# Attention scores: the low parts of the keys on both halves of the partitions, so that both score products read 128 rows

## The chip, the cores and the metric

One core of a Trainium2 chip runs the kernel. The metric is the device time of one execution in microseconds (us). Engines are named as in the profile: PE (TensorE; PEld are its weight loads), DVE (VectorE), ACT (ScalarE), POOL (GpSimd) and SP (SyncE, which issues most transfers).

## What is computed

Two layers of a mixer (convolution and a recurrent scan) with a feed-forward part come first; then a block of attention and a block of 32 experts, of which each token takes four. All data is float32. The change lies in the attention of the second block, over 512 queries and 768 keys (512 tokens and 256 of context). Cut to what matters:

```
scale = d ** -0.5                                    # d = 64
def block(qi):                                       # 8 heads, 2 key heads
    s = jnp.einsum('bhgqd,bkhd->bhgqk', qi, k, preferred_element_type=jnp.float32) * scale
    p = jax.nn.softmax(s, axis=-1)
    return jnp.einsum('bhgqk,bkhd->bqhgd', p.astype(v.dtype), v)
```

There are two kinds of attention: a grouped-query one as above, and a differential one (4 heads), in which two softmaxes of 64 channels each are subtracted, the second times a factor lambda, before the product with the values.

## The kernel before

Queries and keys lie with the channel on the partition: a tile of 128 partitions holds two heads (or the two parts of a differential head) of 64 channels. `s` (or `z`) says which half of the partitions.

PE multiplies in float32r, which keeps fewer bits than float32. So each operand is split into a high part (rounded to float32r) and a low part (what is left). `split_q` makes the tile QS, [128, 2, 512]: for each half `s` the high parts on the half's own 64 partitions and the low parts on the other 64. `split_k` makes KS, [128, 2, 768]: for each half the keys' high parts on both halves of the partitions (two copies, by POOL or, for the first head, by ACT, lines 1475 and 1476), and KL, [128, 768]: the low parts, each half on its own partitions (DVE, line 1477). Both tiles have two buffers.

`softmax` makes the scores of 128 queries against 768 keys, in three pieces of 256 keys, each as two products that add up. The first (line 1488) contracts over 128 rows: high and low queries against high keys. The second (line 1489) contracts over 64 rows: high queries against low keys, `T.matmul(sc[:, N], q[R, s, Q], kl[R, N], ...)`, where R are the half's own partitions. The scores lie in the PSUM tile `sc`, which has two buffers. DVE then takes the least of each row (line 1491; the queries carry -1/8), ACT the exponential with its row sum (line 1494), DVE the reciprocal.

What follows a score step: DVE scales the probabilities P (line 1528, or 1557 and 1558 for a differential head, where two steps are merged), PE transposes them (line 1503, `tp`), ACT copies the transposes into PT (line 1504), and PE multiplies PT with the values into `av` (line 1535 for the grouped-query steps, with 64 columns of weights, line 1565 for the differential heads).

`attention` lists 64 score steps: four differential heads of 8 steps, then four grouped-query steps `j` of 8 steps. What follows a step is emitted three steps later; the scheduler of the framework then orders each engine's instructions. Attention is thus 64 x 6 = 384 score products. A key tile is split five times in all: once for each differential head and once for all grouped-query steps.

Ahead of attention are the products for queries, keys and values; behind it the output projection, the routing, and the experts, whose weights stream from DRAM for the rest of the time.

Of the kernel before, what the change touches and what calls it, by code (L numbers as in the profile page):

```python
# [8 lines left out]
F32 = mybir.dt.float32  # L9
F32R = mybir.dt.float32r  # L10
# [11 lines left out]
DEC = 0.606531  # L22


# ---------------------------------------------------------------- host layout
class Vecs:
    """Per-channel vectors side by side, channel on the partition."""
# [19 lines left out]
def pack_m(w):  # L47
    """[K, M] -> [M/128, 128, K/128 * 128]: the k-tiles of one column block side by side."""
    k, m = w.shape
    return np.ascontiguousarray(  # L50
        w.reshape(k // 128, 128, m // 128, 128).transpose(2, 1, 0, 3).reshape(m // 128, 128, -1))


def host(I):
# [26 lines left out]
    for l in range(2):  # L81
# [8 lines left out]
        up = np.stack([I["decay_up"][l], I["iclr_up"][l]], 0)               # [2, dir, 64, 512]  # L90
# [6 lines left out]
    qa = w[:, :512].reshape(1024, 2, 4, 64).transpose(0, 2, 1, 3).reshape(1024, 512)   # heads (j, 4 + j) side by side  # L97
# [63 lines left out]
def consts():  # L161
    """Depend on shapes alone."""
# [20 lines left out]
# ---------------------------------------------------------------- the kernel  # L183
# [4 lines left out]
class Stat:  # L188
    """sums of squares over the channels, a column per 128 tokens, from tiles as they come"""
# [24 lines left out]
class Kern:  # L214
    def __init__(self, tc, A, pvat, out, dbg=None):
        self.tw, self.narrow = NT, False
        self.tc, self.nc, self.A, self.at, self.out = tc, tc.nc, A, pvat, out
        self.dbg_out = dbg or {}
        self.V, self.S, self.G, self.T = tc.nc.vector, tc.nc.scalar, tc.nc.gpsimd, tc.nc.tensor
        self.moe_ps, self.queue, self.spare, self.wpre = False, None, [], []  # L220
        self.ada_w = 1024
        self.th = ""               # the strand of work that emits: buffers are handed out in order within each
        self.phm, self.ppm, self.psh = {}, {}, {}     # pools of a strand of its own

    # -- small helpers
# [39 lines left out]
    def rsqrt(self, t, n, name):  # L265
        """t[128, n] > 0 -> 1/sqrt(t), by bits and three Newton steps."""
# [15 lines left out]
    def pin(self, ins):  # L282
        """behind what its engine was given before"""
        return self.tc.keep_in_program_order(ins)
# [11 lines left out]
    # -- weights  # L296
# [18 lines left out]
    def dense(self, src, act, segs, done, kts=8, m=128):  # L315
        """out[m, tok] = w^T act in three passes of float32r; done(i, seg, psum)."""
# [14 lines left out]
    def flush(self, g, mid=None):  # L331
        """the products put off: the first g side by side, a term of each in turn; mid: emitted after their weights;
        what it returns: a step of it per term, done before the last"""
# [20 lines left out]
    # -- adaLN: columns of silu(c) @ w + b, both streams  # L354
# [10 lines left out]
    def ada(self, w, cs, bname, mod, groups, pth=None):  # L365
        """mod[128, 48, 2] += for the groups of 2048 columns."""
        for g in groups:
# [15 lines left out]
            # column q*128 + 32 j + s of tp: block 4 j + q of the group, stream s  # L383
# [8 lines left out]
    # -- rms norm and modulation, channel-major  # L392
    def modcols(self, mod, gname, sh, sc, name):
        """a = g (1 + sc), b = sh for both streams: [128, 8, 2]."""
# [5 lines left out]
    def normstat(self, tiles, segs, name):  # L400
        """1 / rms, on all partitions"""
# [18 lines left out]
    def spread(self, r, segs, name):  # L420
        """a column per 128 tokens as rows on all partitions"""
# [10 lines left out]
    def normmod(self, tiles, segs, a, b, name, streams=None, full=False, dst=None, bcs=None, ahead=False):  # L432
        """hi/lo of rms(x) a + b (full: itself, in dst where given)."""
# [43 lines left out]
    def normmod2(self, tiles, ms, g, a, b):  # L477
        """hi/lo of rms(xb) a + b with xb = rms(x) g, over the latents; then xb in x's place.
        rms(xb)'s mean square is that of x g over the mean square of x; ms: both."""
# [35 lines left out]
    # -- group norm over the 64-channel groups of a tile, tokens at the offsets of segs  # L515
    def gn_center(self, t, segs, name, pin=False):
        """t -= group mean (in place)."""
# [7 lines left out]
    def grp_rstd(self, sq, segs, scale, eps, name, floor=None, rb=None):  # L525
        """psum per seg: rsqrt(sum over the tile's two 64-channel groups * scale + eps)."""
# [23 lines left out]
    # -- token shift of width 3  # L550
# [13 lines left out]
    def wi_tile(self, l, mt, segs, name, out=None):  # L564
        """one column block of the RWKV part of u, shifted. mt counts blocks of 128 after the conv part.
        Where the product is put off, what shifts it."""
# [20 lines left out]
    # -- the scan of one head pair, both directions. Per chunk of 64 tokens:  # L587
    #    A, B (alpha with beta, kappa), D, E (rho with beta, kappa), X = (1 + A)^-1,
    #    U = -X (alpha S + B V), y = rho S + D U + E V, S' = f (S + beta U + kappa V);
    #    with W = X alpha and U0 = -X B V that is S' = M S + c, y = R S + y0 where  # L590
    #    M = f (1 - beta W), c = f (beta U0 + kappa V), R = rho - D W, y0 = D U0 + E V
    def units(self, d, q):
        """first chunk of the direction's batch q"""
# [6 lines left out]
    def scan_in(self, l, hp, kvs, kt=None, rt=None, kk=None):  # L600
# [9 lines left out]
        off = (self.ph if hp % 2 else ph).tile([128, 24, 32], F32, name="off", bufs=1)      # rows 0-31, 64-95: the block beside the diagonal  # L610
# [21 lines left out]
        for d in range(2):  # L632
# [15 lines left out]
            V.tensor_scalar(thw, thw, -0.5 * DEC, -0.5 * DEC, op0=ALU.mult, op1=ALU.add)   # log decay  # L648
# [28 lines left out]
            # kappa = Eb k (1 + (a - 1) ka), beta = Eb kk a, a = (1 + tha) / 2  # L677
# [11 lines left out]
            # A, for the reverse direction with alpha's token on the partition; its diagonal 32 x 32 blocks go to  # L689
            # lane 8 b + 4 s + i of quadrant (direction, half)  # L690
# [19 lines left out]
    def scan_inv(self, inv=None):  # L710
# [3 lines left out]
        # inverses of the 32 x 32 blocks, one block to a partition  # L714
# [19 lines left out]
    def scan_x(self, off, G1, G2):  # L734
        V, S, G, T = self.V, self.S, self.G, self.T
        # X transposed: diagonal blocks, and -(T2 A21 T1)^T (forward), -(T1 A12 T2)^T (reverse)
# [34 lines left out]
    def scan_pre(self, l, hp, H):  # L771
        """per chunk M and R (over alpha and rho), c and y0"""
# [8 lines left out]
        def early(q, d):  # L781
# [9 lines left out]
            # the two heads on two halves of the rows, side by side  # L791
# [16 lines left out]
            # f beta and f kappa with the token on the partition  # L808
# [10 lines left out]
            # f on the diagonal in alpha's place  # L819
# [69 lines left out]
    def scan_run(self, l, hp, H):  # L889
        """the recurrence over chunks, both directions in step"""  # L890
# [4 lines left out]
        for q in range(3):  # L895
            full = l == 0 or q > 0
            ub = [self.units(d, q) for d in range(2)]
            # the half of the batch with the smaller chunk numbers first
# [30 lines left out]
    def scan_out(self, l, hp, y, kvs, segs, out=None):  # L929
        """group norm, bonus and gate, in place; the last pair's into out"""  # L930
# [31 lines left out]
    def token_terms(self, l, hp, kt, vt, rt, kvs, segs):  # L962
        """normed removal key, bonus of the current token and gate, to DRAM"""
# [4 lines left out]
        # v with the token on the partition  # L968
# [38 lines left out]
    def conv_z(self, l, ci, segs):  # L1007
        """value * sigmoid(gate) (twice), zero-padded: x at 15, ctx at 557."""
# [26 lines left out]
    def conv_taps(self, l, ci, z, segs, pool):  # L1035
        """the depthwise convolution"""
# [20 lines left out]
    def conv_norm(self, l, ci, tiles, segs, mixd):  # L1057
        """twice the silu of the group norm"""
# [21 lines left out]
    def project(self, l, kvs, mixd, zd, lw):  # L1080
        """w_in and the token shift"""
# [9 lines left out]
        # high and low parts over each other: [hi; lo] of w, [lo; hi] of a  # L1091
# [41 lines left out]
    def conv_diag(self, l, ci, zd, segs, steps):  # L1133
        """the depthwise convolution as products with diagonals, in steps"""
# [76 lines left out]
    def mixer_out(self, l, kvs, mixd, mod, spill):  # L1211
        """x + gt1 (mix @ w_out)"""
# [53 lines left out]
    def ffn(self, l, xt, r2, a2, b2, mod):  # L1266
        """x + gt2 (swiglu), in place; the hidden columns in three parts."""
# [56 lines left out]
    # ------------------------------------------------------------ second block  # L1324
# [4 lines left out]
    def rope(self, t, out, name):  # L1329
        """t [128, 512] of the latents -> out"""  # L1330
# [8 lines left out]
    def head_norm(self, t, segs, g):  # L1339
        """rms over the 64 channels of each head, in place."""  # L1340
# [7 lines left out]
    def ctx_ahead(self, mod):  # L1348
        """the second block's normed context"""
# [8 lines left out]
    def qkv(self, xt, ms, mod):  # L1358
        """x (after the first block's norm), queries, keys and token-major values."""
# [25 lines left out]
        def piped(jobs):  # L1385
            """two products ahead of what follows one"""
# [21 lines left out]
        def lat(i):  # L1408
            def first():
# [4 lines left out]
                self.dense(self.A["wqkv"][i], hx, xs, done)    # 0-3 qa, 4 ka, 5-8 qb, 9-12 kb  # L1414
# [22 lines left out]
    def lambda_col(self):  # L1437
        """[128, 1]: minus lambda"""
# [17 lines left out]
    def split_q(self, q, first=False):  # L1456
        """times -1/8, per head, high parts on its own partitions and low parts on the others"""
# [10 lines left out]
    def split_k(self, k, first=False):  # L1468
        """per head, high parts on both halves of the partitions; low parts"""
        t = self.pqs.tile([128, 2, NT], F32R, name="KS", bufs=2)  # L1470
        lo = self.pqs.tile([128, NT], F32R, name="KL", bufs=2)
        for s in range(2):
# [4 lines left out]
            self.V.tensor_tensor(lo[R], k[R], t[R, s].bitcast(F32), ALU.subtract)  # L1477
        return t, lo

    def softmax(self, q, k, s, qt):  # L1480
        """unnormalised exp of the scores of 128 queries and 1 / row sum; the queries carry -1/8, so that the
        scores' maximum is the least here"""
        V, S, T = self.V, self.S, self.T
        kh, kl = k
        Q, R = slice(qt * 128, (qt + 1) * 128), slice(64 * s, 64 * s + 64)
        sc = self.psc.tile([128, NT], F32, name="sc")       # starts on a bank or in its middle
        for N in (slice(0, 256), slice(256, 512), slice(512, 768)):
            T.matmul(sc[:, N], q[:, s, Q], kh[:, s, N], start=True, stop=False)  # L1488
            T.matmul(sc[:, N], q[R, s, Q], kl[R, N], start=False, stop=True)  # L1489
# [17 lines left out]
    def attention(self, mod):  # L1507
# [3 lines left out]
        steps = []           # (scores and exp, what follows) in order  # L1511
# [108 lines left out]
    def rows_ahead(self, mod):  # L1620
        """scale, shift and gate of the experts' norm as rows in DRAM; the router's part that all tokens share"""
        V, S, G, T, nc, A = self.V, self.S, self.G, self.T, self.nc, self.A
        # the sum of what the experts make of a token, zero at first
# [30 lines left out]
    def out_proj(self, mix, mod):  # L1654
        """Output projection and residual, token-major in Y; what the routing needs of it, as the tiles come:
        the mean squares, and the products with the router's weights before the norm's scale of a token."""
# [793 lines left out]
```

## Time and profile before

| | us |
|---|---|
| three runs | 4617.17, 4621.3, 4623.69 |
| median | 4621.3 |
| profiled execution, first to last instruction | 4622.1 |
| of it PE busy (share) | 4289.2 (93%) |
| DVE busy | 2919.9 (63%) |
| ACT busy | 2070.3 (45%) |
| POOL busy | 963.8 (21%) |

The span of the profiled execution is the one time that is known of it; it lies among the three runs. Busy shares over the whole span mix stages with different limits, so they are read by stage. Attention takes about 287 us of the span.

### The profile page before, as it was taken

What the parts mean: (1) busy time and instruction counts of PE and PEld (TensorE: products, weight loads), DVE (VectorE), ACT (ScalarE), POOL (GpSimd) and SP (SyncE); (2) the same over time, 40 slices, a digit from 0 to 9 for tenths busy, and PEclk for the clock granted to TensorE, in tenths of its full rate; (3) what the DMA queues carried; (4) which work ended last, traced back from release to release, by engine and by line L of the source; (5) the groups of instructions that cost most, each with busy time, mean ns of one, the idle gap of its engine ahead of it and who ended that gap; (6) DMA issues with size and microseconds to landing.
All of it is one profiled execution on the core that took longest, in us unless ns stands there. A gap on an engine that the chain in (4) does not pass through costs nothing.

```text
span 4622.1 us, 68704 instructions
## 1 busy us (share of the span) xinstructions
PE 4289.2 (93%) x26930; PEld 3276.4 (71%) x26930; DVE 2919.9 (63%) x4417; ACT 2070.3 (45%) x3140; POOL 963.8 (21%) x796
## 2 busy tenths in 40 slices
PE   7888999999999888899899999998899999999997
PEld 5664565888888664455788886666777777777775
DVE  6884675433333884755444355645888888888887
ACT  4554332231212553432323242343566666766665
POOL 1552121000000441111000032102323223323222
PEclk9888999999999998889999998798999999999998
DMA  4224323311112224322332241003799989999896
GB/s 157 69 90 128 103 88 107 106 60 64 64 61 80 69 86 134 92 88 84 116 105 92 87 146 41 3 1 126 239 306 305 309 300 303 306 309 304 306 303 244
DMA packets 249438, 691.04 MB, mean 150 GB/s; under 512 B 52055, under 2 KB 60912, under 8 KB 249106
## 3 DMA queue, kind: packets, MB, share of 16 engines
q1 hardware_dynamic: 224354, 636.25, 40.9%
q0 software_dynamic: 7808, 20.74, 1.9%
q10 hardware_dynamic: 16944, 29.58, 1.9%
q8 instruction: 214, 3.51, 0.3%
q14 instruction: 118, 0.97, 0.1%
HBM read 643.12 MB, written 51.45 MB: 150 GB/s over the span
## 4 chain that ended last, share of the span: by engine, by line
PE 42%; DMA 6%; DVE 3%; issue 1%; ACT 1%; POOL 0%; SPq 0%; DVEq 0%; POOLq 0%; ACTq 0%
DMA yd<-ye,ixs 5%; PE dps L326 4%; PE dps L328 4%; PE dps L327 4%; PE acc L1930 4%; PE acc L1931 4%; PE acc L1929 4%; PE acc L1953 3%; PE acc L1954 3%; PE acc L1952 3%; PE tok L1872 2%; PE sc L1489 2%; PE sc L1488 1%; PE av L1535 1%; PE tp L1503 1%; DVE elo L1911 1%
## 5 line engine op out<-in xcount | busy, mean ns | idle before, releaser
L1909 ACT CAST ehi<-eraw 128x1024 fp32r<-128x1024 f32 x768 | 803.1, 1051 | 381.4 <-PE acc L1931 229.3
L1911 DVE TENSOR_TENSOR elo<-eraw,ehi 128x1024 fp32r<-128x1024 f32 x640 | 865.3, 1390 | 97.7 <-ACT ehi L1909 95.5
L309 ACT CAST whi<-wraw 128x1024 fp32r<-128x1024 f32 (+1 forms) x234 | 239.5, 1028 | 768.1 <-PE dps L327 416.0
L1911 POOL TENSOR_TENSOR elo<-eraw,ehi 128x1024 fp32r<-128x1024 f32 x128 | 331.3, 2588 | 847.8 <-ACT ehi L1909 771.8
L310 DVE TENSOR_TENSOR wlo<-wraw,whi 128x1024 fp32r<-128x1024 f32 (+1 forms) x234 | 292.2, 1251 | 225.6 <-ACT whi L309 222.3
L1930 PE MATMUL acc<-elo,ex 128*128 128x512 f32 x1024 | 416.0, 406 | 14.4 <-DVE elo L1911 13.2
L1929 PE MATMUL acc<-ehi,ex 128*128 128x512 f32 x1024 | 408.7, 399 | 0.3 <-ACT ex L1875 0.3
L1931 PE MATMUL acc<-ehi,ex 128*128 128x512 f32 x1024 | 408.0, 398 | 0.0
L327 PE MATMUL dps<-h2l,whi 128*128 128x512 f32 x992 | 351.2, 354 | 0.0
L326 PE MATMUL dps<-h2h,whi 128*128 128x512 f32 x992 | 351.1, 354 | 0.0
L328 PE MATMUL dps<-h2h,wlo 128*128 128x512 f32 x992 | 350.3, 353 | 0.0
L1930 PEld LDWEIGHTS acc<-elo,ex 128*128 128x128 f32 x1024 | 194.7, 190 | 65.4 <-DVE elo L1911 20.6
L376 PE MATMUL adaps<-wraw,cs 128*32 128x512 f32 x576 | 234.6, 630 | 2.8 <-DMA wraw<-in_ada_dram 1.8
L1929 PEld LDWEIGHTS acc<-ehi,ex 128*128 128x128 f32 x1024 | 194.7, 190 | 47.3 <-issue 0.7
L328 PE MATMUL dps<-hh,wlo 128*128 128x512 f32 (+3 forms) x568 | 209.5, 370 | 17.6 <-DVE wlo L310 17.6
L1931 PEld LDWEIGHTS acc<-ehi,ex 128*128 128x128 f32 x1024 | 194.6, 190 | 39.3
L326 PE MATMUL dps<-hh,whi 128*128 128x512 f32 (+3 forms) x568 | 210.4, 370 | 5.5 <-ACT whi L309 4.9
L1953 PE MATMUL acc<-elo,eah 128*128 128x512 f32 x512 | 206.9, 404 | 1.7 <-DVE elo L1911 1.7
L326 PEld LDWEIGHTS dps<-h2h,whi 128*128 128x128 f32 x992 | 188.0, 190 | 26.4
L327 PE MATMUL dps<-hl,whi 128*128 128x512 f32 (+3 forms) x568 | 206.8, 364 | 0.0
L1952 PE MATMUL acc<-ehi,eah 128*128 128x512 f32 x512 | 203.5, 397 | 3.3 <-DVE ye L1972 3.3
L328 PEld LDWEIGHTS dps<-h2h,wlo 128*128 128x128 f32 x992 | 187.8, 189 | 26.1
(605 smaller groups left out, 9508.8 us busy)
## 6 DMA issues: line engine op xcount, KB each, us to landing
eraw<-in_ewi_dram SPq DMA_DIRECT2D x503, 512.0 KB, 6.0
eraw<-in_ewo_dram SPq DMA_DIRECT2D x256, 512.0 KB, 5.2
wraw<-in_ada_dram SPq DMA_DIRECT2D x256, 256.0 KB, 2.9
wraw<-in_wi_dram SPq DMA_DIRECT2D x44, 512.0 KB, 3.8
wraw<-in_wg_dram SPq DMA_DIRECT2D x44, 512.0 KB, 3.7
wraw<-in_wu_dram SPq DMA_DIRECT2D x44, 512.0 KB, 3.7
wraw<-in_wd_dram SPq DMA_DIRECT2D x32, 512.0 KB, 3.7
wraw<-in_wqkv_dram SPq DMA_DIRECT2D x28, 512.0 KB, 3.7
```

The source lines that it names most:

```text
L309: self.S.copy(hi, raw)
L310: i = self.V.tensor_tensor(lo, raw, hi.bitcast(F32), ALU.subtract)
L326: self.T.matmul(ps, w0, h[:, o:o + n], start=k == 0, stop=False)
L327: self.T.matmul(ps, w0, l[:, o:o + n], start=False, stop=False)
L328: self.T.matmul(ps, w1, h[:, o:o + n], start=False, stop=k == kts - 1)
L1909: self.S.copy(hi, raw)
L1911: (self.G if self.wn % 6 == 0 else self.V).tensor_tensor(lo, raw, hi.bitcast(F32), ALU.subtract)
L1929: T.matmul(acc[:, N], xh[:, K], wh[:, W], start=False, stop=False)
L1930: T.matmul(acc[:, N], xh[:, K], wl[:, W], start=False, stop=False)
L1931: T.matmul(acc[:, N], xl[:, K], wh[:, W], start=False, stop=k == 7)
L1952: T.matmul(acc[:, N], ah[:, K], wh[:, N], start=k == 0, stop=False)
L1953: T.matmul(acc[:, N], ah[:, K], wl[:, N], start=False, stop=False)
```

## The change

DVE now writes the low parts of the keys on both halves of the partitions: KL becomes [128, 2, 768], and in place of one subtraction of 64 partitions per half there are two with the same inputs, one for each place. The second score product reads all 128 rows of QS and KL, so that it also adds low queries against low keys. The rest of the difference drops comments and moves line numbers: from line 1478 on, a line of the changed kernel is one higher than in the kernel before (the products at lines 1488 and 1489 stand at 1489 and 1490, the subtraction at 1478).

```
     def split_k(self, k, first=False):
         t = self.pqs.tile([128, 2, NT], F32R, name="KS", bufs=2)
-        lo = self.pqs.tile([128, NT], F32R, name="KL", bufs=2)
+        lo = self.pqs.tile([128, 2, NT], F32R, name="KL", bufs=2)
         for s in range(2):
             R, N = slice(64 * s, 64 * s + 64), slice(64 - 64 * s, 128 - 64 * s)
             C = lambda e: self.S.copy if e else self.G.tensor_copy
             C(first)(t[R, s], k[R])
             C(False)(t[N, s], k[R])
-            self.V.tensor_tensor(lo[R], k[R], t[R, s].bitcast(F32), ALU.subtract)
+            for P in (R, N):
+                self.V.tensor_tensor(lo[P, s], k[R], t[R, s].bitcast(F32), ALU.subtract)
         return t, lo
...
         kh, kl = k
-        Q, R = slice(qt * 128, (qt + 1) * 128), slice(64 * s, 64 * s + 64)
+        Q = slice(qt * 128, (qt + 1) * 128)
...
             T.matmul(sc[:, N], q[:, s, Q], kh[:, s, N], start=True, stop=False)
-            T.matmul(sc[:, N], q[R, s, Q], kl[R, N], start=False, stop=True)
+            T.matmul(sc[:, N], q[:, s, Q], kl[:, s, N], start=False, stop=True)
```

How the instructions stand now, in two places. DVE at the start of attention, before the change (QS and KL are the split queries and keys, `nb` the row minimum, `wlo` a weight of the output projection that is prepared early):

```order
L1465 SCALAR_TENSOR_TENSOR QS<-q_22701,QS 64x512 x2
L1477 TENSOR_TENSOR KL<-k_22706,KS 64x768 x2
L310 TENSOR_TENSOR wlo<-wraw,whi 128x1024
L1491 TENSOR_REDUCE nb<-sc 128x1
L310 TENSOR_TENSOR wlo<-wraw,whi 128x1024
L1491 TENSOR_REDUCE nb<-sc 128x1
L1465 SCALAR_TENSOR_TENSOR QS<-q_22702,QS 64x512
```

The same place in the changed kernel:

```order
L1465 SCALAR_TENSOR_TENSOR QS<-q_22701,QS 64x512 x2
L1478 TENSOR_TENSOR KL<-k_22706,KS 64x768 x4
L310 TENSOR_TENSOR wlo<-wraw,whi 128x1024 x2
L1492 TENSOR_REDUCE nb<-sc 128x1
L1465 SCALAR_TENSOR_TENSOR QS<-q_22702,QS 64x512
L1492 TENSOR_REDUCE nb<-sc 128x1
L1465 SCALAR_TENSOR_TENSOR QS<-q_22702,QS 64x512
```

The first key tile's four subtractions stand ahead of the first reduction, where there were two, and the second weight has moved ahead of the first reduction.

PE near the end of the second differential head, before (`sc` the scores, `tp` the transposes, `av` the product with the values):

```order
L1488 MATMUL sc<-KS,QS 128x256
L1489 MATMUL sc<-KL,QS 128x256
L1503 MATMUL tp<-ct,P 128x128 x3
L1565 MATMUL av<-PT,vtok 128x256 x3
L1503 MATMUL tp<-ct,P 128x128 x3
L1565 MATMUL av<-PT,vtok 128x256 x3
L1488 MATMUL sc<-KS,QS 128x256
L1489 MATMUL sc<-KL,QS 128x256
```

The same place in the changed kernel:

```order
L1489 MATMUL sc<-KS,QS 128x256
L1490 MATMUL sc<-KL,QS 128x256
L1566 MATMUL av<-PT,vtok 128x256 x6
L1504 MATMUL tp<-ct,P 128x128 x6
L1489 MATMUL sc<-KS,QS 128x256
L1490 MATMUL sc<-KL,QS 128x256
```

The same products stand there, but those with the values come as one group ahead of the transposes rather than in two groups between them; the score products keep their pairs.

## Rows read from the trace of the kernel before

**Rows 1.** The page's first line: the whole span.

```profile
span 4622.1 us, 68704 instructions
```

**Rows 2.** Busy time by stage: length, each engine, granted clock, DMA share, GB/s.

```profile
2846.00:3018.00 172.00, 155.81 (x493) 106.64 (x491) 103.60 (x195) 64.13 (x130) 28.75 (x25) 0.68 0.04 11
3018.00:3133.00 115.00, 115.00 (x518) 70.53 (x518) 54.12 (x105) 52.20 (x115) 12.46 (x16) 0.97 0.04 12
...
3205.00:3330.00 125.00, 99.30 (x468) 81.07 (x468) 99.51 (x112) 65.40 (x87) 53.19 (x24) 0.86 0.53 174
3330.00:4590.00 1260.00, 1214.53 (x5690) 976.81 (x5690) 1045.45 (x949) 861.27 (x978) 377.30 (x151) 0.99 0.90 307
```

**Rows 3.** The chain of waits, 2840 to 3135 us, shares by line.

```profile
by line: PE sc L1489 23.7%; PE sc L1488 20.5%; PE av L1535 15.4%; PE tp L1503 15.4%; PE av L1565 12.4%; PE tp L1589 2.0%; ACT P L1494 2.0%; DVE nb L1491 1.3%; PE tp L1580 1.2%; DVE QS L1465 0.9%; PE dps L328 0.6%; ACT PT L1504 0.6%; PE dps 
```

**Rows 4.** DVE's groups, 2846 to 3018 us: busy, mean ns, idle before, releaser.

```profile
L1491 DVE TENSOR_REDUCE nb<-sc 128x1 f32<-128x768 f32 x38 | 36.4, 958 | 61.3 <-PE sc L1489 61.2
...
L1477 DVE TENSOR_TENSOR KL<-k,KS 64x768 fp32r<-64x768 f32 x10 | 10.9, 1086 | 0.2
```

**Rows 5.** PE in order of time, second half: start us, length us, instruction.

```profile
3047.89 0.38 PE L1489 MATMUL sc<-KL,QS 64*128 64x256 f32 x1
3048.20 0.39 PE L1488 MATMUL sc<-KS,QS 128*128 128x256 f32 x1
3048.52 0.38 PE L1489 MATMUL sc<-KL,QS 64*128 64x256 f32 x1
```

**Rows 6.** PE in order of time, dense products ahead of attention, full clock.

```profile
2721.03 0.28 PE L328 MATMUL dps<-hch,wlo 128*128 128x256 f32 x1
2721.15 0.28 PE L326 MATMUL dps<-hch,whi 128*128 128x256 f32 x1
2721.27 0.28 PE L327 MATMUL dps<-hcl,whi 128*128 128x256 f32 x1
```

**Rows 7.** PE in order of time, first half, half clock.

```profile
2910.75 0.58 PE L1489 MATMUL sc<-KL,QS 64*128 64x256 f32 x1
2911.26 0.58 PE L1488 MATMUL sc<-KS,QS 128*128 128x256 f32 x1
2911.77 0.58 PE L1489 MATMUL sc<-KL,QS 64*128 64x256 f32 x1
```

**Rows 8.** PE in order of time, dense products behind attention, half clock.

```profile
3222.27 1.65 PE L1872 MATMUL tok<-ohs,hr 128*128 128x256 f32 x6 [1.92 <-POOL hr L1780]
```

**Rows 9.** The second score products by half: length, PE, PEld, clock, DMA share, GB/s.

```profile
2846.00:3018.00 172.00, 54.80 (x114) 26.68 (x114) 0.68 0.04 11
3018.00:3133.00 115.00, 29.89 (x78) 14.36 (x78) 0.97 0.04 12
```

**Rows 10.** Who waited for whom, 2845 to 3135 us: total us, times, longest.

```profile
POOL eraw L1667 <- PE sc L1489: 64.0, 1, 64.0
```

**Rows 11.** The instructions on the scores: ns least/median/most, first and last start.

```profile
L1494 ACT ACTIVATE P<-sc,nb x64: 892/902/924, 2855.6 to 3127.4; 128x768 f32<-128x768 f32 x64
L1494 ACT ACTIVATION_READ_ACCUMULATOR P<-sc,nb x64: 191/193/220, 2856.4 to 3128.2; 128x1 f32 x64
```

**Rows 12.** The chain of waits in order of time, end of attention.

```profile
3135.47 2.80 PE av L1535 x12
```

**Rows 13.** Busy time in slices around a group of dense products; columns as before.

```profile
2898.00:2901.00 3.00, 3.00 (x8) 2.37 (x9) 2.85 (x6) 0.99 (x2) 0.00 (x0) 0.50 0.00 0
...
2903.00:2906.00 3.00, 3.00 (x15) 1.87 (x14) 0.95 (x1) 1.68 (x4) 0.00 (x0) 0.96 0.00 0
2906.00:2910.00 4.00, 4.00 (x23) 2.97 (x23) 2.08 (x11) 2.76 (x8) 0.00 (x0) 1.00 0.00 0
2910.00:2914.00 4.00, 4.00 (x9) 2.24 (x9) 1.10 (x3) 0.27 (x1) 0.00 (x0) 0.51 0.00 0
```

**Rows 14.** PE in order of time: that group of dense products.

```profile
2897.82 5.49 PE L1565 MATMUL av<-PT,vtok 128*128 128x256 f32 x12
```

More of the change, by code (lines that the diff above doesn't have):

```diff
@@ L1470, in split_k @@
         t = self.pqs.tile([128, 2, NT], F32R, name="KS", bufs=2)
-        lo = self.pqs.tile([128, NT], F32R, name="KL", bufs=2)
+        lo = self.pqs.tile([128, 2, NT], F32R, name="KL", bufs=2)
         for s in range(2):
@@ L1476, in split_k @@
             C(False)(t[N, s], k[R])
-            self.V.tensor_tensor(lo[R], k[R], t[R, s].bitcast(F32), ALU.subtract)
+            for P in (R, N):
+                self.V.tensor_tensor(lo[P, s], k[R], t[R, s].bitcast(F32), ALU.subtract)
         return t, lo
@@ L1484, in softmax @@
         kh, kl = k
-        Q, R = slice(qt * 128, (qt + 1) * 128), slice(64 * s, 64 * s + 64)
+        Q = slice(qt * 128, (qt + 1) * 128)
         sc = self.psc.tile([128, NT], F32, name="sc")
@@ L1488, in softmax @@
             T.matmul(sc[:, N], q[:, s, Q], kh[:, s, N], start=True, stop=False)
-            T.matmul(sc[:, N], q[R, s, Q], kl[R, N], start=False, stop=True)
+            T.matmul(sc[:, N], q[:, s, Q], kl[:, s, N], start=False, stop=True)
         nb = self.small("nb", 1)
```

## Prediction

> **What bounds the kernel now.** I first read the span [rows 1] and then busy times by stage [rows 2]. The stage of the change is attention, from about 2846 to 3133 us, 287 of the 4622.1 us. The reader is to see two halves in it. In the first (four differential heads, 172 us) PE is busy for 155.8, DVE for 103.6 and ACT for 64.1, and the granted clock is 0.68 of full. In the second (four grouped-query steps, 115 us) PE is busy all the time, DVE for 54.1 and ACT for 52.2, at a clock of 0.97. DMA does almost nothing in either. So PE bounds the stage, and the chain of waits says the same: the two score products alone are 23.7% and 20.5% of it there [rows 3]. DVE's largest group waits: its 38 row reductions of the first half were idle for 61.2 us until the second score product was done [rows 4].
>
> Then I read how far apart score products start. At full clock (a product lasts 0.38 us) one starts 0.31 us after the other, the 128-row one and the 64-row one alike [rows 5]. A dense product with the same moving size (128x256, fp32r, weights loaded anew each time, 128 rows every time) starts 0.12 us after the one before it [rows 6]. At half clock (a product lasts 0.58 us) the score products are 0.51 apart [rows 7]; of six 128-row products of 256 columns at half clock, the group takes 1.65 us, so (1.65 - 0.58) / 5 = 0.21 apart [rows 8]. What differs is that the score products alternate between 128 and 64 rows. I read the missing 0.19 us (full clock) and 0.30 us (half) as PE emptying itself at each change of row count, after which the next weight load and product start.
>
> How much is at which clock: 114 second products in the first half take 54.80 us, 0.481 each, half way between 0.38 and 0.58, so half of them ran at half clock; in the second half 78 take 29.89 us, 0.383 each, so nearly all ran at full clock [rows 9].
>
> **The change, part by part.** (1) The second score product reads 128 rows, so row counts no longer change between the 384 score products. If PE stays the bound and the clock stays as it is: first half 228 products, 114 x 0.19 + 114 x 0.30 = 56 us; 172 - 56 = 116. Second half 156 products. Of these I leave 16 out, those ahead of the 16 groups of P times V, whose weights are 128*64: the array's shape changes there still, and no row tells that this costs nothing. 140 x 0.19 = 27; 115 - 27 = 88. With all 156 it would be 85.
>
> (2) DVE makes the low parts of a key tile four times rather than twice: 10 more instructions at 1.086 us, 10.9 us [rows 4], all of them in the first half. DVE's work there becomes 103.6 + 10.9 = 114.5 us. That is a floor for the first half, nearly as high as PE's 116. The cover for the added work is DVE's idle time (61.2 us), which the change itself takes away. So the added work isn't free any more: each us of it that is late delays the reduction behind it, that delays the exponential on ACT, and that the release of one of the two score buffers, for which PE waits. Two of the added instructions stand ahead of the first score at all, with nothing beside them: 2 us.
>
> In the first half neither engine now clearly covers the other. I take 120 us: 116, those 2 us, and 2 more, chosen, for steps in which each waits for the other. The floor is DVE's 114.5. Second half: 88 us, where DVE and ACT stay below 55.
>
> (3) The larger tile KL takes 3 KB more per partition in each of its two buffers; no transfer runs in this stage that it could delay. The first loads for the expert stage are issued by POOL when the last score is done (a wait of 64.0 us ends with it [rows 10]), so they move with the end of the stage. The low queries now also meet low keys; that is arithmetic in the same product and costs nothing.
>
> (4) Order. The scheduler shifts a few transposes and P times V groups by one step among the score products and puts DVE's two added rows per half behind the first two. PE's number of score products, transposes and P times V is unchanged. I cost the shifts at nothing: the pieces are the same, and up to two scores stand ready ahead. If that cover is gone, one step waits for reduction and exponential, 0.96 + 0.90 + 0.19 us [rows 4, 11], a few times; that is inside the range.
>
> (5) Behind attention everything waits for it: the chain runs from its last P times V products, to 3138 us, into the output projection [rows 12], and the stages up to 3330 us follow each other on PE, DVE and POOL. From 3330 us on DMA is 0.90 busy at 307 GB/s [rows 2], fed by loads that begin only at the end of attention. So the whole tail moves as one, and I count a gain in attention in full.
>
> Sum: 172 + 115 = 287 us become 120 + 88 = 208, 79 us less. The profiled execution took 4622.1 us, so 4543; it lies 0.8 us above the median of the three runs, so **4542 us**, 1.7% faster.
>
> **A rule against it.** Rows 5 show 64-row products one after the other, 0.31 us apart, though 64 rows leave half of the array free. The Trainium skill (TensorEngine Tiling, "When to Use Tiling") says the opposite of what the change does: a contraction of 64 is to be split into two row tiles that work at once, for up to twice the speed. By it a 64-row product would cost half a 128-row one, and making it 128 rows would lose 192 x 0.06 = 11.5 us against an ideal pairing. In this kernel the 64-row products alternate with 128-row ones and never run in pairs, so by the rows the sum stays as above.
>
> **The rivals.** *The first half isn't paced by DVE or PE alone, but by the clock.* In the first half the clock falls from 1.00 to 0.51 behind a slice in which PE runs scores and transposes, and rises to 0.96 in the slice behind twelve dense P times V products [rows 13, 14]. After the change the scores are denser, which speaks for a higher clock; but PE will wait for DVE more, which speaks against. If the first half ran at half clock throughout: PE's work without scores is 155.8 - 114 x (0.31 + 0.51) = 62 us at a clock of 0.68, so 62 x 0.68 / 0.5 = 84 at half; scores 228 x 0.21 = 48; together 132, and with the waits of the 32 steps (about 0.4 us each, as a guess between nothing and 0.96) 145. Then 145 + 88 = 233, 54 us saved: 4567.
>
> *The clock falls in the second half too*, the other side. PE's work there without scores is 115 - 156 x 0.31 = 67 us at full clock, 134 at half, and scores 156 x 0.21 = 33: 167 us in place of 115. With 132 in the first half that is 299, 12 us more than now: 4633. It decides from about 0.87 of the stage at half clock (208 + 0.87 x 91 = 287). Against it: the second half keeps a clock of 0.97 now, with less dense work. For it is a rule of the Trainium skill (TensorE: Matmul & The Clock Gate, "Why this matters for your kernels"): idle gaps between bursts of products bring the clock to its lower level. The trace agrees only in the first half, where PE has 16 us of idle time [rows 2].
>
> *The row count isn't what costs 0.19 us.* The dense products also differ in that they add 24 terms into one tile, the scores 2. If that were it, the products stay 0.31 apart, DVE's 10.9 us hide in its idle time, and 2 us at the start are added: 4623, no change. Against it: both orders, 128 to 64 and 64 to 128, cost the same [rows 5].
>
> *Better than forecast*: 114.5 + 85, and the last 0.03 of clock (3 us) back: 197, 90 us less, 4531.
>
> **How the numbers follow.** Chances: forecast with its neighbours down to 4531 0.68, clock in the first half (4555 to 4575) 0.2, no change 0.06, both halves slow 0.03, and 0.03 for a gain that is partly lost behind the stage. The range 4530 to 4570 goes from the floor of both halves to the first rival and leaves out under 0.2. What can be told from no change here is 0.2%, 9 us. Faster 0.92, same 0.05, slower 0.03.
>
> **What would show it.** Right: second score products of 128*128 that start 0.12 us apart (0.21 at half clock); DVE's wait for the scores down from 61.2 us in the first half to under 20; first half 115 to 125 us, second 85 to 90; stages behind it as long as before. Wrong: products still 0.31 apart; a clock under 0.6 in the first half; or a later stage that is longer by what attention gained.

## The result, and the profile after

The changed kernel takes 4538.53 us (median of 4 runs, 4535.81 to 4542.59) against 4620.89 us of the kernel before: a ratio of 0.9822, with an interval of 0.9807 to 0.9836. That is 82 us less; 79 were forecast, and 4542 us. The page of the profiled execution begins:

```profile
span 4537.9 us, 68718 instructions
```

Its span is 84.2 us shorter than in [rows 1]. To see where these come from, attention is cut at the same events in both traces: from the first score product to the first product of a grouped-query step with the values (first half), and from there to the end of the last (second half). The kernel before, busy time by half (columns as in [rows 2]):

```profile
2849.50:3018.20 168.70, 155.37 (x488) 106.40 (x488) 102.24 (x194) 60.70 (x124) 25.43 (x22) 0.68 0.03 8
3018.20:3138.30 120.10, 119.86 (x540) 73.28 (x540) 53.92 (x105) 53.53 (x118) 12.46 (x16) 0.97 0.08 28
```

The changed kernel, the same two stretches:

```profile
2850.00:2967.40 117.40, 86.89 (x489) 78.39 (x489) 108.88 (x204) 59.59 (x123) 27.59 (x22) 0.81 0.04 12
2967.40:3057.70 90.30, 89.90 (x540) 63.26 (x539) 53.73 (x105) 53.30 (x120) 12.52 (x16) 1.00 0.11 36
```

The first half lost 51.3 us, the second 29.8, and the rest of the span 3.1. The reader is to look at the engines' columns. In the second half PE is still busy all the time: it bounds it as before, with less to do. In the first half PE fell from 155.4 to 86.9 us, and DVE is now busy for 108.9 of 117.4: the bound has moved to DVE. The granted clock rose in both halves.

PE in order of time in the second half of the changed kernel (L1489 and L1490 are the two score products):

```profile
3014.15 0.36 PE L1489 MATMUL sc<-KS,QS 128*128 128x256 f32 x1
3014.35 0.28 PE L1490 MATMUL sc<-KL,QS 128*128 128x256 f32 x1
3014.47 0.28 PE L1489 MATMUL sc<-KS,QS 128*128 128x256 f32 x1
3014.59 0.28 PE L1490 MATMUL sc<-KL,QS 128*128 128x256 f32 x1
3014.71 0.28 PE L1489 MATMUL sc<-KS,QS 128*128 128x256 f32 x1
3014.83 0.28 PE L1490 MATMUL sc<-KL,QS 128*128 128x256 f32 x1
3014.95 0.82 PE L1504 MATMUL tp<-ct,P 128*128 128x128 f32 x6
```

The score products now start 0.12 us apart, as the dense ones in [rows 6] did, and not 0.31 [rows 5]; only the first after the transposes takes 0.20. A product also lasts 0.28 us rather than 0.38. At half clock, in the first half, they start 0.21 apart, and not 0.51 [rows 7]:

```profile
2862.12 0.41 PE L1490 MATMUL sc<-KL,QS 128*128 128x256 f32 x1
2862.33 0.41 PE L1489 MATMUL sc<-KS,QS 128*128 128x256 f32 x1
```

DVE's groups in the first half of the changed kernel (busy, mean ns, idle before):

```profile
L1492 DVE TENSOR_REDUCE nb<-sc 128x1 f32<-128x768 f32 x38 | 35.8, 949 | 5.9 <-PE sc L1490 5.7
L1478 DVE TENSOR_TENSOR KL<-k,KS 64x768 fp32r<-64x768 f32 x20 | 21.3, 1065 | 0.3
```

The reductions' wait for the scores, 61.2 us in [rows 4], is down to 5.7. And the chain of waits over the first half, by line, starts with DVE where the two score products led in [rows 3]:

```profile
by line: DVE nb L1492 12.8%; DVE KL L1478 7.8%; DVE P L1559 6.7%; PE av L1566 5.8%; ACT P L1495 4.8%; DVE P L1558 4.6%; PE sc L1489 3.7%; DVE QS L1465 2.9%; POOL QS L1464 2.8%; PE sc L1490 2.8%; issue 2.3%; PE tp L1504 2.2%; PE tp L1590 1.8
```

### The profile page after: what moved, and what is told of

It reads as the page before. It is cut to its first block, busy times and chain, and to the rows that moved or that the text cites. A ratio compares the mean times of both kernels' runs of the same rounds, so it can differ in the third digit from the quotient of the medians.

```text
span 4537.9 us, 68718 instructions
## 1 busy us (share of the span) xinstructions
PE 4187.2 (92%) x26930; PEld 3237.4 (71%) x26930; DVE 2924.9 (64%) x4427; ACT 2070.1 (46%) x3140; POOL 968.1 (21%) x796
## 5 line engine op out<-in xcount | busy, mean ns | idle before, releaser
L1931 PEld LDWEIGHTS acc<-elo,ex 128*128 128x128 f32 x1024 | 194.2, 190 | 65.5 <-DVE elo L1912 22.2
L327 PEld LDWEIGHTS dps<-h2l,whi 128*128 128x128 f32 x992 | 188.2, 190 | 25.8
```

The source lines that it names most:

```text
L327: self.T.matmul(ps, w0, l[:, o:o + n], start=False, stop=False)
L1931: T.matmul(acc[:, N], xh[:, K], wl[:, W], start=False, stop=False)
```

## The experiments

Theory A: a change of row count costs PE 0.19 us at full clock and 0.30 us at half clock, whichever way it goes. Rival B: the 64-row product, or a sum of two terms, is slow by itself. For what bounds the kernel now there are two more: DVE's work paces the first half, or PE and its clock do. The first four kernels ran beside each other on one chip, where the kernel before took 4621.37 us, the other four on another, where it took 4624.52. The profiled runs reached the first score between 2843.9 and 2861.1 us, though what stands ahead of it is the same in all, but for some 4 us of zeros that POOL writes in two of them. What is left of the span beside attention varied from 4324.9 to 4344.6 us. So attention tells more than whole times where a few us matter. There is one trace of each kernel; the changed kernel, which has two, gave 117.4 and 116.0 us for its first half and 90.3 twice for its second.

**Four changes of row count per step.** The edit to the kernel before:

```
-            T.matmul(sc[:, N], q[:, s, Q], kh[:, s, N], start=True, stop=False)
-            T.matmul(sc[:, N], q[R, s, Q], kl[R, N], start=False, stop=True)
+            H, W = (q[:, s, Q], kh[:, s, N]), (q[R, s, Q], kl[R, N])
+            one, two = (W, H) if N.start == 256 else (H, W)
+            T.matmul(sc[:, N], one[0], one[1], start=True, stop=False)
+            T.matmul(sc[:, N], two[0], two[1], start=False, stop=True)
```

> The kernel before, with the 64-row product ahead of the 128-row one in the middle piece of 256 keys, so that a step of six score products has four changes of row count in place of six; same tiles, same work on DVE. Theory A (a change of row count costs PE 0.19 us at full clock and 0.30 us at half): a third of 56 and 30 us is saved, 28 us, so 4593 us, and of neighbours with equal rows the second starts 0.12 us later. Rival B (the 64-row product, or a sum of two terms, is slow by itself): 4621 us and 0.31 us everywhere.

Measured: 4586.66 us, ratio 0.9916 (0.99 to 0.9931). One step of it, PE in order of time:

```profile
3060.81 0.36 PE L1490 MATMUL sc<-KS,QS 128*128 128x256 f32 x1
3061.11 0.38 PE L1491 MATMUL sc<-KL,QS 64*128 64x256 f32 x1
3061.33 0.28 PE L1490 MATMUL sc<-KL,QS 64*128 64x256 f32 x1
3061.53 0.39 PE L1491 MATMUL sc<-KS,QS 128*128 128x256 f32 x1
3061.76 0.28 PE L1490 MATMUL sc<-KS,QS 128*128 128x256 f32 x1
3061.97 0.38 PE L1491 MATMUL sc<-KL,QS 64*128 64x256 f32 x1
3062.28 1.51 PE L1537 MATMUL av<-PT,vtok 128*64 128x256 f32 x6
```

The step takes 1.47 us against 6 x 0.31 = 1.86 before. Theory A holds, with one miss in detail: neighbours with equal rows are 0.22 us apart and not 0.12, and the product after them follows in 0.20, so a pair takes 0.42 to 0.44 and not 0.12 + 0.31. The price of a change is spread over the products on both sides of it; their sum is as expected. 28 us were forecast, 35 came. The first half alone gave 27.5 (to 141.2 us), where the granted clock was 0.74 and not 0.68.

**Two changes per step.** The three 128-row products of a step come first, then the three 64-row ones:

```
         for N in (slice(0, 256), slice(256, 512), slice(512, 768)):
-            T.matmul(sc[:, N], q[:, s, Q], kh[:, s, N], start=True, stop=False)
+            T.matmul(sc[:, N], q[:, s, Q], kh[:, s, N], start=True, stop=False, skip_group_check=True)
+        for N in (slice(0, 256), slice(256, 512), slice(512, 768)):
-            T.matmul(sc[:, N], q[R, s, Q], kl[R, N], start=False, stop=True)
+            T.matmul(sc[:, N], q[R, s, Q], kl[R, N], start=False, stop=True, skip_group_check=True)
```

> The kernel before, with the three 128-row products of a step first and then the three 64-row ones: two changes of row count per step in place of six. Theory A: two thirds of the 86 us, 57 us, so 4564 us, and 0.12 us between neighbours of one kind. Rival B: 4621 us, with 0.31 us between the 64-row products.

Measured: 4549.43 us, ratio 0.9833 (0.9818 to 0.9848). In this order three sums are open beside each other in one PSUM tile, and what the kernel returns is no longer right (why was not looked into), so it is read for its time alone. One step:

```profile
3041.87 0.60 PE L1488 MATMUL sc<-KS,QS 128*128 128x256 f32 x3
3042.40 0.62 PE L1490 MATMUL sc<-KL,QS 64*128 64x256 f32 x3
3042.95 0.33 PE L1504 MATMUL tp<-ct,P 128*128 128x128 f32 x1
```

1.08 us a step. With 0.80 for the changed kernel, steps with 6, 4, 2 and no changes take 1.86, 1.47, 1.08 and 0.80 us: 0.39 for two changes, 0.19 to 0.20 for each. The last two give 0.28 only; the step without changes still starts with 0.20 behind the transposes in place of 0.12. Theory A is shown at full clock; at half clock the changed kernel's 0.21 in place of 0.51 gives the 0.30. In whole time 57 us were forecast and 72 came, and the granted clock in the first half was 0.75: in both kernels more came than the changes alone are worth, and the clock rose with it.

**Both products on 64 rows.** The first score product becomes `T.matmul(sc[:, N], q[R, s, Q], kh[R, s, N], ...)`.

> The kernel before, with the first score product cut to 64 rows too (this leaves out low queries against high keys), so that all score products have 64 rows and none has 128. Theory A: no change of row count within a step, 0.12 us apart at full clock; the first half falls from 172 us to between 104 (DVE's work) and 116, the second to 85 to 90: about 4535 us. Rival B (64 rows are slow by themselves): 4621 us or more, 0.31 us apart. If rows that stand idle let the clock fall, the first half's granted clock is under 0.68.

Measured: 4539.54 us, ratio 0.9821 (0.9806 to 0.9836). One step in its second half, and its two halves:

```profile
3031.78 0.38 PE L1488 MATMUL sc<-KS,QS 64*128 64x256 f32 x1
3032.00 0.28 PE L1489 MATMUL sc<-KL,QS 64*128 64x256 f32 x1
3032.12 0.28 PE L1488 MATMUL sc<-KS,QS 64*128 64x256 f32 x1
3032.24 0.27 PE L1489 MATMUL sc<-KL,QS 64*128 64x256 f32 x1
3032.36 0.28 PE L1488 MATMUL sc<-KS,QS 64*128 64x256 f32 x1
3032.48 0.28 PE L1489 MATMUL sc<-KL,QS 64*128 64x256 f32 x1
3032.68 0.55 PE L1503 MATMUL tp<-ct,P 128*128 128x128 f32 x3
```

```profile
2848.40:2959.40 111.00, 96.81 (x482) 78.72 (x482) 98.20 (x191) 57.88 (x120) 26.09 (x22) 0.75 0.04 12
2959.40:3057.50 98.10, 96.62 (x546) 65.02 (x546) 54.84 (x108) 54.78 (x123) 12.30 (x16) 1.00 0.08 27
```

Rival B falls: 64-row products are 0.12 us apart too when nothing else stands between them, and it is a sum of two terms as before. It is not the 128 rows that pay, but that the rows stay the same. A change remains at either end of each step, ahead of the transposes and behind them; DVE's added work is gone. Attention as a whole takes 209.1 us, the changed kernel's 207.7. (Its halves don't compare with those of the changed kernel: the cut falls behind 37 score steps here and behind 38 there.) The clock in the first half is 0.75, below the changed kernel's 0.81 but above 0.68.

**DVE's added work alone.** The kernel before with the new `split_k`, and `kl[R, s, N]` in the second product.

> The kernel before, with DVE's ten added subtractions and the larger KL, but with the second product still on 64 rows. If DVE's added 10.9 us are hidden wherever PE bounds the first half: 4621 to 4624 us (2 to 3 us at the start). If they aren't hidden: 4632 us.

Measured: 4621.99 us, ratio 1.0001 (0.9989 to 1.0012). First half, and its reductions:

```profile
2845.70:3014.80 169.10, 156.00 (x488) 105.79 (x488) 109.85 (x204) 60.31 (x124) 27.07 (x22) 0.66 0.03 8
```

```profile
L1492 DVE TENSOR_REDUCE nb<-sc 128x1 f32<-128x768 f32 x38 | 36.3, 955 | 46.6 <-PE sc L1490 46.4
```

The first half is 0.4 us longer than in the kernel before: DVE is busy for 7.6 us more, and its wait for the scores is down by 15 us. While PE bounds the half, the added work is hidden. So it costs time only once the gain that it buys has been made.

**DVE's work, less and more.** The changed kernel once more, as the standard:

> The changed kernel once more, as the standard for the runs beside it: 4538 us.

Zeros in place of the second copy, written once; of `split_k`:

```
-        lo = self.pqs.tile([128, 2, NT], F32R, name="KL", bufs=2)
+        if not hasattr(self, "kls"):
+            self.kls = [self.pqs.tile([128, 2, NT], F32R, name=f"KL{i}", bufs=1) for i in range(2)]
+            for z in self.kls:
+                for s in range(2):
+                    N = slice(64 - 64 * s, 128 - 64 * s)
+                    self.G.tensor_copy(z[N, s].rearrange("p (a b) -> p a b", b=128),
+                                       self.zero[N][:, None, :].to_broadcast([64, 6, 128]))
+        lo = self.kls[0]
+        self.kls.reverse()
...
-            for P in (R, N):
-                self.V.tensor_tensor(lo[P, s], k[R], t[R, s].bitcast(F32), ALU.subtract)
+            self.V.tensor_tensor(lo[R, s], k[R], t[R, s].bitcast(F32), ALU.subtract)
```

> The changed kernel, with zeros in place of the second copy of the low keys (this leaves out low queries against low keys, as the kernel before does). The zeros are written once, by POOL, into two tiles that are used in turn, so DVE's ten added subtractions are gone, and all score products still read 128 rows. If DVE now paces the first half: some 6 of its 10.9 us come off the first half, 4532 us. If PE and the clock pace it: 4538 us. The second half stays at 90 us in both.

Ten more subtractions: `for P in (R, N, N):`.

> The changed kernel, with one of the two subtractions of each half done twice: ten more instructions on DVE that no result needs, all in the first half. If DVE paces the first half: 8 to 11 us more, about 4548 us. If it doesn't: 4538 us.

With zeros, and the subtractions of all tiles but the first on POOL: `(self.V if first else self.G).tensor_tensor(lo[R, s], ...)`.

> As the one with zeros, and the subtractions of all key tiles but the first are made by POOL, which takes 8 more instructions off DVE, some 8 us. If DVE still paces the first half: 5 us less than with zeros alone, about 4527 us. If PE and the chain of a step now pace it: the same as with zeros alone. If POOL is late with the low keys, PE waits for KL and it is slower.

| | median us | ratio (interval) | first half | DVE busy in it | score steps in it | second half |
|---|---|---|---|---|---|---|
| changed, again | 4537.76 | 0.9817 (0.9804 to 0.983) | 116.0 | 109.0 | 38 | 90.3 |
| zeros | 4532.63 | 0.9805 (0.9792 to 0.9819) | 105.6 | 97.6 | 37 | 92.9 |
| DVE, ten more | 4555.76 | 0.9856 (0.9841 to 0.9871) | 130.2 | 121.3 | 40 | 88.8 |
| zeros and POOL | 4541.76 | 0.9815 (0.9799 to 0.9831) | 111.4 | 98.3 | 38 | 91.5 |

The rows of the first half, in this order, each from its own trace, and below each the sum over both halves:

```profile
2847.40:2963.40 116.00, 86.34 (x489) 77.74 (x489) 108.99 (x204) 59.57 (x123) 27.33 (x22) 0.81 0.04 12
...
sum 206.30, PE 176.25 PEld 141.00 DVE 162.75 ACT 112.91 POOL 39.84; mean PE 88.12 PEld 70.50 DVE 81.38 ACT 56.45 POOL 19.92
```

```profile
2849.50:2955.10 105.60, 81.96 (x482) 73.44 (x482) 97.59 (x189) 55.14 (x117) 34.03 (x27) 0.86 0.04 13
...
sum 198.50, PE 173.04 PEld 137.53 DVE 151.64 ACT 109.74 POOL 46.31; mean PE 86.52 PEld 68.76 DVE 75.82 ACT 54.87 POOL 23.15
```

```profile
2843.90:2974.10 130.20, 86.38 (x493) 77.60 (x493) 121.25 (x219) 60.39 (x126) 27.91 (x22) 0.81 0.03 11
...
sum 219.00, PE 174.69 PEld 140.60 DVE 172.32 ACT 112.22 POOL 40.01; mean PE 87.35 PEld 70.30 DVE 86.16 ACT 56.11 POOL 20.01
```

```profile
2861.10:2972.50 111.40, 84.74 (x480) 75.60 (x480) 98.25 (x183) 56.53 (x119) 49.56 (x35) 0.83 0.04 12
...
sum 202.90, PE 175.63 PEld 139.51 DVE 152.72 ACT 110.39 POOL 61.85; mean PE 87.81 PEld 69.75 DVE 76.36 ACT 55.19 POOL 30.93
```

In the first three the first half is DVE's busy time and 7 to 9 us, whichever way the work is moved, while PE's work hardly changes: DVE paces it. The sizes can't be read from the first half, since the cut doesn't fall behind the same score step in each; they are read from both halves together. With zeros attention is 7.8 us shorter (198.5 against 206.3), where 6 were forecast. Of these, 3 us are merely moved ahead of the cut: POOL's zeros put off the first score, which starts 4.6 us after DVE's first split of queries (L1465) and not 1.6. Counted from that split, 4.8 us are gained. With ten more subtractions attention is 12.7 us longer (219.0), where 8 to 11 were forecast. Whole times agree in sign: 5 us less, with intervals that overlap, and 18 us more.

POOL's version missed its forecast of 4527. Attention takes 4.4 us longer than with zeros alone (202.9 against 198.5); whole times are 9 us longer, with intervals that overlap. DVE makes eight subtractions fewer, yet is as busy: 152.7 us in attention against 151.6. Two of its groups with zeros alone, then with POOL's help, and POOL's own:

```profile
L1566 DVE SCALAR_TENSOR_TENSOR P<-P,rs 128x768 f32<-128x768 f32 x16 | 17.7, 1109 | 0.2
L1565 DVE TENSOR_SCALAR P<-P,rs 128x768 f32<-128x768 f32 x16 | 10.9, 680 | 0.3
```

```profile
L1566 DVE SCALAR_TENSOR_TENSOR P<-P,rs 128x768 f32<-128x768 f32 x16 | 19.9, 1243 | 0.1
L1565 DVE TENSOR_SCALAR P<-P,rs 128x768 f32<-128x768 f32 x16 | 12.0, 751 | 0.3
```

```profile
L1485 POOL TENSOR_TENSOR KL<-k,KS 64x768 fp32r<-64x768 f32 x8 | 15.4, 1928 | 0.6
```

POOL needs 1.93 us where DVE needs some 1.08, and DVE's own instructions grow meanwhile: by 3.3 us in the two groups shown, by 5.1 in two more (L1564 from 3.2 to 5.3 us, L1732 from 2.7 to 5.7). That is nearly all of the eight subtractions, some 8.7 us: what was taken off DVE comes back on it. The Trainium skill (SBUF — State Buffer, "Who interferes with whom") says that a DVE instruction with two inputs in SBUF contends with a POOL instruction that reads SBUF; the merge of P at L1566 has two such inputs, and its 1109 to 1243 ns agree. L1565 has one tile as its input and grew as well, from 680 to 751 ns, which that sentence doesn't cover. That this sharing is the whole loss was not tried.

## Why the prediction was right, step by step

- *Price of a change of rows, 0.19 us (0.30 at half clock).* Right, and that the change of row count is what costs, too: the time goes with the number of changes over 6, 4, 2 and none, and 64 rows without a change are as quick as 128. That the array drains at a change is my reading; the Trainium skill (TensorEngine Tiling, "Key Properties") says that a change of tiling mode drains TensorE, and the four step lengths agree.
- *First half 172 to 120 us.* From score to first grouped-query product it went from 168.7 to 117.4: 51.3 off, 52 forecast. The number was met partly by luck. Its main term, 116, holds only "if PE stays the bound and the clock stays as it is", and neither did. PE's 155.8 us of work less 56 would have been 100, with 16 us of idle time beside it; 86.9 are left, DVE leads alone, and the half is DVE's 108.9 us and 8.5 more. That DVE's floor lay close to 116 is what made the sum come out; that "neither engine now clearly covers the other" was put too evenly. The further 13 us of PE's work came off with the clock, from 0.68 to 0.81: the 96 products with the values, which the change doesn't touch, took 37.5 us before (first row) and take 24.8 now:

```profile
2849.50:3018.20 168.70, 37.47 (x96) 27.55 (x96) 0.68 0.03 8
```

```profile
2850.00:2967.40 117.40, 24.82 (x96) 19.31 (x96) 0.81 0.04 12
```

- *DVE's floor of 114.5.* Over-sized: 108.9 us were busy. The 20 subtractions cost 21.3 us as reckoned, 10.4 more than before; DVE's other work came out 3.8 us shorter in busy time. Added up one by one its other instructions take 1.1 us less (97.8 to 96.7); the rest is that neighbours overlap in the profile, and now, with fewer pauses between them, by 9.1 us rather than 6.3. The prediction's 103.6 also began 3.5 us ahead of the first score, which is 1.4 us of the difference.
- *Second half 115 to 88, 27 off.* 29.8 came off, nearer the bound of 85. From each start on PE to the next, the score products took 48.4 us before and 22.3 now: 26.1 less, so the 27 was right. The other 3.6 came on products that the change doesn't touch, those with the values (48.3 to 45.8) and the transposes (23.3 to 22.2), as the granted clock went from 0.97 to 1.00. That is the term that was left out: the prediction had it at 3 us, in its best case alone. The 16 products that it left out of the 27 got back 0.10 us each; in the changed kernel the first of these two rows is followed by the second in 0.21 us, not in 0.31:

```profile
3021.83 0.28 PE L1490 MATMUL sc<-KL,QS 128*128 128x256 f32 x1
3022.04 1.51 PE L1536 MATMUL av<-PT,vtok 128*64 128x256 f32 x6
```

- *Two us at the start.* The first reduction began 5.1 us after the first score before and 7.6 us after it now; right, with half a us more.
- *The tail moves as one.* The rest of the span went from 4333.3 to 4330.2 us, within what it varies by. Right.
- *Rivals.* The clock didn't fall: 0.81 and 1.00 in place of 0.68 and 0.97, though PE is idle for 30.5 us of the first half where it was idle for 13.3. The rule of the Trainium skill that was named for this rival (TensorE: Matmul & The Clock Gate, "Why this matters for your kernels"), that idle gaps lower the clock, did not decide here. Nor does it alone account for the kernel before: at 2910 us the clock fell behind 7 us in which the profile shows PE busy without a break [rows 13]. The half-clock case is one that no run reached. "The row count isn't what costs" is refuted by the kernel with 64 rows throughout. Pairs of 64-row products on the two halves of the rows, the rule against the change, were not tried.

## What to carry to other kernels

A short product beside one of another row count pays for the change, here more than for its own work (0.19 us beside 0.12); make all products of a stream alike, even if half the rows multiply zeros. Zeros that are written once give the same shape as a second copy, and took 5 us less here (the intervals overlap), since the engine that made the copy was next in line. Before an engine is relieved, add up what the next one will need: its idle time was the cover for the added work, and it is gone with the gain.

## What the runs showed of the hardware that I had not expected

The price of a row change isn't paid at one place: in the kernel with four changes, two 64-row products in a row are 0.22 us apart and the next product follows 0.20 later, so that equal neighbours next to a change are not at 0.12. And the granted clock was higher although the engine was idle for longer: PE's busy share of the first half fell from 92% to 74% (155.37 of 168.7, 86.89 of 117.4), and the granted clock rose from 0.68 to 0.81. It was higher too with four changes a step (0.74), with two (0.75) and with 64 rows throughout (0.75), and in the kernel with DVE's added work alone, which keeps all six changes, it was not (0.66). Which property of the stream the clock follows was not tried.
